# Where the load buffers start: 384 bytes left free ahead of them, and a first load divided at 3968 columns

## The chip, the cores and the metric

The kernel runs on one core of a Trainium2 chip. The metric is the device time of one execution in microseconds; lower is better. Ratios are computed as the mean time of one kernel's fast runs over the mean of the other's fast runs of the same rounds, so they are not quite the ratio of the medians quoted beside them.

## The reference

A cross entropy with label smoothing over 256 rows of 32000 float32 logits, 32.77 MB in all:

```python
log_probs = logits - np.max(logits, axis=-1, keepdims=True)
log_probs = log_probs - np.log(np.sum(np.exp(log_probs), axis=-1, keepdims=True))
# smooth_targets: smoothing / num_classes everywhere, 1 - smoothing more at the label
return (-np.sum(smooth_targets * log_probs, axis=-1)).astype(np.float32)
```

For each row it takes the sum of the logits, the sum of their exponentials and the one logit at the label.

## The kernel before

Each of the 128 partitions holds two rows ("row 0" and "row 1" below). They are loaded in 14 pieces; VectorE sums the logits of a piece and ScalarE its exponentials. Large pieces go into a ring of three buffers of 32000 bytes per partition, small ones into buffers of their own right behind the ring.

```python
WIDTHS = (
    (8000, 8000, 8000, 8000),
    (8000, 6272, 4736, 3648, 2688, 2048, 1536, 1216, 1024, 832),
)
# ...
    ring = ctx.enter_context(tc.tile_pool(name="ring", bufs=3))
    tail = ctx.enter_context(tc.tile_pool(name="tail", bufs=1))
# ...
    def load(w: int, col: int, name: str):
        # ... xt from ring (w >= 4736) or tail
        if col == 0:
            h = w // 2
            nc.sync.dma_start(out=xt[:, :h], in_=x[:, :h])
            nc.scalar.dma_start(out=xt[:, h:w], in_=x[:, h:w])
        else:
            nc.sync.dma_start(out=xt[:, :w], in_=x[:, col : col + w])
        return xt
# ...
        nc.scalar.activation(out=ja[:, :w], in_=xt[:, :w], func=AF.Exp, accum_out=out)
```

A load is 128 descriptors, one per partition, each a contiguous run of up to 32000 bytes; each of the 16 DMA engines carries 8 of them. "A row" below, where DMA is meant, is one such descriptor.

The softmax here doesn't subtract the row's maximum and nothing guards it: scores larger than these inputs give would overflow.

## Time and profile before

| what | value |
|---|---|
| median of 3 runs | 84.77 us (84.75 to 84.93) |
| span of the profiled execution | 83.2 us |
| DMA queues of the loads, share of 16 engines' span | 87.4% + 5.8% |
| ScalarE, VectorE busy | 71%, 45% |
| first byte of the loads moved, last byte moved, last load landed | 1.04, 78.66, 79.11 us |
| last exponential starts | 79.24 us |

How to read it: the DMA engines work without a break from 1.04 to 78.66 us. After the last landing only a short chain is left: the last exponential, its logarithm, a transpose on TensorE, a sum on VectorE, and the store. "Landed" means that the last of the load's 16 engines has reported.

### The profile page before, as it was taken

The page shows a single profiled execution, that of the slowest core. Times are in us where ns is not written, and L with a number is a line of the kernel's source. Part 1 is how long each engine was busy: PE and PEld are TensorE (multiplying, and loading weights), DVE is VectorE, ACT ScalarE, POOL GpSimd, SP SyncE. Part 2 cuts the span into 40 slices and gives each one's busy share as a digit, 9 for nine tenths or more (in the row PEclk, how much of TensorE's full clock was granted, in tenths as well). Part 3 has the DMA queues.
Part 4 walks back from the last instruction along what each step waited for, and adds up shares of the span by engine and source line. Part 5 has one row for each costly group of instructions (what it writes and reads, how often), then busy time and mean ns, then how long its engine had stood idle before and what let it go on. Part 6 is the DMA issues. An engine that isn't in the chain of part 4 may idle for free.

```text
span 83.2 us, 230 instructions
## 1 busy us (share of the span) xinstructions
PE 7.0 (8%) x23; PEld 5.0 (6%) x23; DVE 37.1 (45%) x35; ACT 58.8 (71%) x31; POOL 5.7 (7%) x19
## 2 busy tenths in 40 slices
PE   0000000000000000000000010000000000899020
PEld 0000000000000000000000000000000000787000
DVE  0000005950495009910397017922944736754860
ACT  5000005997499809994399908997999999999960
POOL 3201640031000000000000040000000000000000
PEclk9999999999999999999999999999999999999995
DMA  5999999997999899989998998998999999999600
GB/s 131 416 416 408 454 423 462 477 447 323 477 493 431 369 431 493 446 369 416 493 462 354 416 439 386 495 447 370 428 420 414 442 407 415 412 414 412 256 0 0
DMA packets 2258, 32.77 MB, mean 394 GB/s; under 512 B 337, under 2 KB 338, under 8 KB 850
## 3 DMA queue, kind: packets, MB, share of 16 engines
q1 hardware_dynamic: 2018, 30.72, 87.4%
q10 hardware_dynamic: 144, 2.05, 5.8%
q0 software_dynamic: 96, 0.00, 0.1%
HBM read 32.77 MB, written 0.00 MB: 394 GB/s over the span
## 4 chain that ended last, share of the span: by engine, by line
DMA 64%; ACT 32%; issue 1%; SPq 0%; PE 0%; DVE 0%; ACTq 0%
DMA xt<-in_logits_dram 40%; DMA xl<-in_logits_dram 23%; ACT ja L188 17%; ACT jt L188 15%; SPq L167 0%; PE lse_t L193 0%; DVE res L284 0%; ACT lse L279 0%; ACTq L188 0%
## 5 line engine op out<-in xcount | busy, mean ns | idle before, releaser
L188 ACT ACTIVATE ja<-xt 128x8000 bf16<-128x8000 f32 (+2 forms) x7 | 43.9, 6276 | 20.1 <-DMA xt<-in_logits_dram 20.0
L173 DVE SCALAR_TENSOR_TENSOR jd<-xt 128x4000 f32<-128x4000 f32 (+2 forms) x7 | 27.7, 3954 | 33.6 <-DMA xt<-in_logits_dram 33.6
L188 ACT ACTIVATE jt<-xl 128x3648 bf16<-128x3648 f32 (+6 forms) x7 | 12.2, 1748 | 0.1
L173 DVE SCALAR_TENSOR_TENSOR jd<-xl 128x1824 f32<-128x1824 f32 (+6 forms) x7 | 7.9, 1125 | 5.2 <-DMA xl<-in_logits_dram 5.0
L270 PE MATMUL warm<-xl,ident 128*128 128x256 f32 x20 | 6.1, 471 | 21.4 <-DMA xl<-in_logits_dram 21.4
L270 PEld LDWEIGHTS warm<-xl,ident 128*128 128x128 f32 x20 | 4.8, 246 | 22.5 <-DMA xl<-in_logits_dram 21.7
L193 PE MATMUL loss_t<-ident,loss 128*1 128x128 f32 x1 | 0.4, 372 | 49.2 <-POOL loss L224 49.2
L193 PEld LDWEIGHTS loss_t<-ident,loss 128*1 128x1 f32 x1 | 0.1, 79 | 49.2 <-POOL loss L224 49.2
L226 DVE COPY res<-loss_t 1x128 f32<-1x128 f32 x1 | 0.3, 278 | 4.5 <-PE loss_t L193 4.5
L211 POOL TENSOR_TENSOR half<-sums 128x4 f32<-128x4 f32 x1 | 0.2, 198 | 28.2 <-ACT ja L188 28.2
L125 POOL DMA_INDIRECT gat<-in_logits_dram,flat_idx x2 | 2.0, 1004 | 0.7 <-POOL ident masks.py:199 0.4
L92 ACT ACT_TABLE_LOAD x1 | 1.3, 1283 | 0.9 <-PEq L311 0.9
L188 ACT ACTIVATION_READ_ACCUMULATOR ja<-xt 128x1 f32 x7 | 1.3, 186 | 0.0
L188 ACT ACTIVATION_READ_ACCUMULATOR jt<-xl 128x1 f32 x7 | 1.3, 181 | 0.0
L146 POOL TENSOR_SCALAR weighted<-gat 128x1 f32<-128x1 f32 x1 | 0.8, 763 | 5.8 <-DMA gat<-in_logits_dram,flat_idx 5.8
L105 POOL DMA_DIRECT2D lab<-in_labels_dram x1 | 0.8, 766 | 1.0 <-POOLq L311 1.0
L216 ACT ACTIVATE lse<-half 128x1 f32<-128x1 f32 x1 | 0.2, 203 | 0.6 <-POOL half L211 0.6
L173 DVE DVE_READ_ACCUMULATOR jd<-xt 128x1 f32 x7 | 0.6, 82 | 0.0
L173 DVE DVE_READ_ACCUMULATOR jd<-xl 128x1 f32 x7 | 0.6, 82 | 0.0
L117 POOL TENSOR_TENSOR flat_idx<-rowoff,lab 128x2 int32<-128x2 int32 x1 | 0.2, 197 | 5.4 <-DMA lab<-in_labels_dram 5.4
L193 PE MATMUL lin_t<-ident,done 128*1 128x128 f32 x1 | 0.3, 270 | 3.0 <-DVE done L263 3.0
L282 DVE COPY lin_row<-lin_t 1x128 f32<-1x128 f32 x1 | 0.3, 278 | 0.4 <-PE lin_t L193 0.4
(20 smaller groups left out, 3.8 us busy)
## 6 DMA issues: line engine op xcount, KB each, us to landing
xt<-in_logits_dram SPq DMA_DIRECT2D x4, 4000.0 KB, 21.1
xt<-in_logits_dram SPq DMA_DIRECT2D x1, 3136.0 KB, 19.4
xt<-in_logits_dram SPq DMA_DIRECT2D x1, 2368.0 KB
xt<-in_logits_dram SPq DMA_DIRECT2D x1, 2000.0 KB, 11.5
xt<-in_logits_dram ACTq DMA_DIRECT2D x1, 2000.0 KB, 13.2
xl<-in_logits_dram SPq DMA_DIRECT2D x1, 1824.0 KB, 19.5
xl<-in_logits_dram SPq DMA_DIRECT2D x1, 1344.0 KB, 22.3
xl<-in_logits_dram SPq DMA_DIRECT2D x1, 1024.0 KB, 24.3
```

The source lines that it names most:

```text
L92: nc.scalar.add_instruction(mybir.InstLoadActFuncSet(name=nc.get_next_instruction_name(), act_func_set_id=tbl, ins=[], outs=[],))
L105: nc.gpsimd.dma_start(out=lab[:], in_=labels.bitcast(I32).rearrange("(p f) -> p f", p=P))
L117: nc.gpsimd.tensor_tensor(out=flat_idx[:], in0=rowoff[:], in1=lab[:].rearrange("p (r two) -> p r two", two=2)[:, :, 0:1], op=ALU.add,)
L125: nc.gpsimd.indirect_dma_start(out=gat[:, r : r + 1], out_offset=None, in_=logits[:], in_offset=bass.IndirectOffsetOnAxis(ap=flat_idx[:, r ...
L146: nc.gpsimd.tensor_scalar(out=weighted[r], in0=gat[:, r : r + 1], scalar1=label_weight, scalar2=None, op0=ALU.mult,)
L173: return nc.vector.scalar_tensor_tensor(out=jd[:, :h], in0=xt[:, :h], scalar=1.0, in1=xt[:, h:w], op0=ALU.mult, op1=ALU.add, accum_out=out,)
L188: nc.scalar.activation(out=ja[:, :w], in_=xt[:, :w], func=AF.Exp, accum_out=out)
L193: nc.tensor.transpose(out=row[:], in_=column, identity=ident[:])
L211: nc.gpsimd.tensor_tensor(out=half[:], in0=sums[:, :, :n], in1=sums[:, :, n:], op=ALU.add)
L226: nc.vector.tensor_copy(out=res[:, :, r : r + 1], in_=loss_t[:])
L270: nc.tensor.matmul(warm[:], lhsT=ident[:], rhs=xt[:, i * WARM_COLS : (i + 1) * WARM_COLS], start=True, stop=True,)
L282: nc.vector.tensor_copy(out=lin_row[:], in_=lin_t[:])
```

## The change

Its intent is to let every descriptor of the large loads start on a multiple of 256 bytes, in SBUF and in DRAM. In the built program the ring began at byte 16512 of each partition (64.5 x 256); with 384 bytes of padding ahead of it, it begins at 16896 (66 x 256). The first load was cut at 16000 bytes (62.5 x 256), and is now cut at 15872 (62 x 256).

```diff
+PAD = 384
@@
+    pad = ctx.enter_context(tc.tile_pool(name="pad", bufs=1))
+    pad.tile([nc.NUM_PARTITIONS, PAD // 4], FP32, name="pad", tag="pad")
     ring = ctx.enter_context(tc.tile_pool(name="ring", bufs=3))
@@
-            h = w // 2
+            h = w // 128 * 64
```

## The prediction

> **What bounds the kernel now.** I read the page's span and slices first, then the chain of waits, then the timeline of the last 35 us, then busy times in chosen stretches, and last the packet records of the trace (one per descriptor: start, duration, size). The slices put the 16 DMA engines at nine tenths or more nearly everywhere:
>
> ```profile
> DMA  5999999997999899989998998998999999999600
> ...
> q1 hardware_dynamic: 2018, 30.72, 87.4%
> q10 hardware_dynamic: 144, 2.05, 5.8%
> ```
>
> The two queues of the loads fill 87.4 + 5.8 = 93.2% of 83.15 us, 77.5 us on each engine. By the packet records the first byte of the loads moves at 1.04 us and the last ends at 78.66 us, a stretch of 77.6 us: the DMA engines have no idle time to give back. Only the time per descriptor could shrink. The chain of waits shows who hands over to whom at the end (columns: start us, length us, what):
>
> ```profile
> 20.35 20.37 DMA xt<-in_logits_dram
> 40.72 0.02 issue
> 40.74 0.02 ACTq L188
> 40.76 0.04 issue
> 40.80 6.97 ACT ja L188 x2
> ...
> 48.17 19.52 DMA xl<-in_logits_dram
> 67.69 0.02 issue
> 67.72 7.63 ACT jt L188 x5
> ```
>
> Up to 67.69 us the landing of loads sets the pace; from 67.72 us on ScalarE does, without a pause, until 80.2 us. The timeline shows how close the two are (start, duration, instruction, in brackets the idle time before it):
>
> ```profile
> 50.31 6.87 ACT L188 ACTIVATE ja<-xt 128x8000 bf16<-128x8000 f32 x1 [1.75 <-DMA xt<-in_logits_dram]
> ...
> 57.77 5.43 ACT L188 ACTIVATE ja<-xt 128x6272 bf16<-128x6272 f32 x1 [0.50 <-DMA xt<-in_logits_dram]
> ...
> 63.41 4.15 ACT L188 ACTIVATE ja<-xt 128x4736 bf16<-128x4736 f32 x1
> ...
> 67.72 3.24 ACT L188 ACTIVATE jt<-xl 128x3648 bf16<-128x3648 f32 x1
> ...
> 70.96 2.44 ACT L188 ACTIVATE jt<-xl 128x2688 bf16<-128x2688 f32 x1
> ```
>
> Set beside them when each load landed, by the trace's semaphore records: the 3648-column load landed at 67.69 us and its exponential began at 67.72; for the six that follow the pairs are 70.94 and 70.96, 73.42 and 73.44, 75.31 and 75.39, 76.82 and 76.90, 78.10 and 78.18, 79.11 and 79.24. The widths were tuned so that each load lands just as ScalarE needs it. A DMA that gets faster therefore meets ScalarE at once.
>
> The rate of the DMA in stretches that hold one load size each (columns: stretch, its length, busy time and instructions of PE, weight loads, DVE, ACT, POOL, then clock, DMA share, GB/s):
>
> ```profile
> 21.00:49.00 28.00, 0.00 (x0) 0.00 (x0) 13.00 (x6) 21.09 (x7) 0.82 (x5) 1.00 0.99 427
> ...
> 67.30:69.90 2.60, 0.00 (x0) 0.00 (x0) 2.07 (x2) 2.54 (x3) 0.00 (x0) 1.00 0.98 414
> ...
> 74.90:75.80 0.90, 0.90 (x6) 0.77 (x6) 0.40 (x1) 0.90 (x3) 0.00 (x0) 1.00 1.01 410
> ```
>
> The engines are full in all three, and the rate falls as rows get shorter (32000, 10752, 4864 bytes): each descriptor carries something fixed besides its bytes.
>
> **What the Trainium skill says.** "DMA: Bandwidth & Descriptors", section "Where 436 GB/s comes from", gives 16 ports x 32 bytes x 850 MHz = 435 GB/s. The trace agrees: between rows of 8192 and 25088 bytes the median duration rises from 313 to 935 ns, 622 ns for 16896 bytes or 528 beats of 32 bytes, 1.178 ns a beat, which is 849 MHz. So no change of addresses can lift the rate above about 435, and the large loads already run at 427. Section "How a descriptor splits into AXI transactions" says that a descriptor which starts on a 256-byte boundary goes out as pieces of 256 bytes, and that one which doesn't starts its first piece at the boundary below, whose unused bytes still cost beats. "SBUF — State Buffer", section "SBUF: two separate sides", says that DMA and engines use disjoint ports, so I expect no effect of moved addresses on compute; no run here shows that yet.
>
> **The change part by part.** The order of instructions on every engine is the same in both builds, with the same sizes except for the two first transfers. So nothing is removed or added; only addresses move. In the built program the load buffers begin at byte 16512 of each partition, 128 bytes past a multiple of 256. With the pad they begin at 16896, a multiple of 256 (and of 512). The other ring buffers lie 32000 bytes apart (125 x 256), and all widths of row 1 are multiples of 64 columns (256 bytes), so before, every load's destination sat 128 bytes off, and after, every one is aligned. The sources in DRAM were aligned already, but for the first load's second half (16000 bytes is 62.5 x 256), which the division at 3968 (62 x 256 bytes) mends. After it the two parts are 62 and 63 whole pieces.
>
> What is an off-boundary descriptor charged? A row of n pieces that starts 128 bytes off touches n + 1 of them. If each touched piece takes a full 8 beats, a descriptor takes 8(n+1) beats. I took durations in beats (1.176 ns) from the packet records: 25088 bytes (n = 98) takes 935 ns = 794.8, against 8 x 99 = 792; 18944: 709 ns = 602.7 against 600; 14592: 549 = 466.7 against 464; 10752: 408 = 346.8 against 344; 8192: 313 = 266.1 against 264; 4864: 191 = 162.4 against 160; 16000 (63 pieces touched on either half): 596 = 506.6 against 504; 32000: 1186 = 1008.1 against 1008. One rule with a rest of 2 to 3 beats (none at 32000) fits halves and whole rows alike. A plain "bytes plus a constant" needs 10.7 beats at 14592 but 6.6 at 16000. I take the rule of touched pieces, as my estimate. Aligned, each row then saves one piece, 8 beats = 9.4 ns.
>
> Each engine has 8 rows of every load, so each load saves 8 x 9.4 = 75 ns; the divided first load saves one piece for each pair of halves, also 75 ns. The saving at the landing of each load adds up: first load 0.08 us, fifth load (row 1's 8000 columns) 0.38, 6272 columns 0.45, 4736 columns 0.53, 3648 columns 0.60, 2688 columns 0.68, 2048 columns 0.75, the last (832) 14 x 0.075 = 1.05. (These are 14 loads; the last lands at 79.11 - 1.05 = 78.06.)
>
> What ScalarE makes of it, carrying its own durations: 8000 columns begin at 50.31 - 0.38 = 49.93 and end about 56.8. The 6272 columns land for 57.77 - 0.45 = 57.32 and end at 62.75. The 4736 columns begin at 63.41 - 0.53 = 62.88 and end at 67.03. The 3648 columns begin at 67.72 - 0.60 = 67.12. The 2688 columns would have landed for 70.28, but ScalarE is free only at 67.12 + 3.24 = 70.36. From there ScalarE alone sets the end; its seven activations follow on one another as before, and the gain stays at 0.60 us plus whatever of the waits of 0.02 to 0.06 us between them goes, at most 0.1. The remaining 0.45 us of DMA time is gained where no one waits for it. Sum: 84.77 - 0.60 to 0.70 = 84.1 to 84.2 us.
>
> **The rivals.** First, a fixed cost: the 6 to 10 beats per row could be what any descriptor costs, aligned or not. For it: every row before the change starts off a boundary on one side, so nothing in this trace shows an aligned one. Against it: the misfit of 16000 against 14592 bytes above. It would leave 84.77. Second, half of it: if the cut first and last pieces together are charged only 4 beats extra, the saving at the 3648-column load is 0.30 us, and the time 84.45. Third, the whole saving reaches the end, were ScalarE not there: 84.77 - 1.05 = 83.7. Against it: ScalarE's unbroken row from 67.72 us. Fourth, the pad moves the buffers that the engines write and read, and slows VectorE or ScalarE; nothing speaks for it, and a loss of 1% in ScalarE's 12.5 us tail is 0.13 us. A large gain is excluded by the beat: if every beat beyond the bytes went up to the 3648-column load (6.6 for each half, 8 for 32000 bytes, 10.7 for three later sizes, 8 rows each), that is 8 x (13.2 + 32 + 32.1) = 618 beats = 0.73 us.
>
> **Range and chances.** I give the touched pieces two chances in three, half of it and the fixed cost the rest, and lean a little towards them: 84.2 us, and 83.9 to 84.8 eight times in ten. Faster by over 2% would need 83.1 us, more than the whole saving of the DMA: 2%. Slower by over 2%: 1%. Within 2%: 97%.
>
> **What would show it.** Packet durations: 32000-byte rows at 1176 to 1179 ns instead of 1186, 25088 at 926 instead of 935, 4864 at 181 instead of 191; the halves at about 586 and 596. The rate in the large loads near 430 to 433. The loads' last packet about 1.05 us earlier, near 77.6; the 3648-column exponential at 67.1, and VectorE in the tail starting before ScalarE on the same tile, as its data is there sooner. ScalarE's durations unchanged (6870 ns for 8000 columns). Wrong if durations stay (fixed cost), if rows shorten but another gap opens between them, or if any activation gets longer.

## The result, and the profile after

84.34 us (median of 6, 84.28 to 84.56) against 84.78 (median of 6 of the same rounds): ratio 0.9951, 95% interval 0.9937 to 0.9966. That is a gain of 0.44 us, clear of noise and inside 2%. It lies inside the predicted range; the point forecast was 84.2.

The page's lines for the DMA, after: as full as before, the same shares of a span that is 0.6 us shorter.

```profile
span 82.6 us, 230 instructions
...
DMA  5999999996999799979997999998999999999600
...
q1 hardware_dynamic: 2018, 30.71, 87.4%
q10 hardware_dynamic: 144, 2.06, 5.9%
```

The chain of waits, after (start, length, what). Compare 67.72 and 67.31 for the first piece of the tail, and the shape of what follows:

```profile
57.45 5.52 ACT ja L194 x2
...
63.05 4.24 ACT ja L194 x2
...
67.31 7.53 ACT jt L194 x5
74.83 0.06 issue
74.89 1.40 ACT jt L194
76.29 0.07 issue
76.36 1.22 ACT jt L194 x2
```

The five entries that took 7.63 us before take 7.53. ScalarE looked unbroken before, but it had been stretched by pauses of hundredths of a microsecond. By the instruction records these were 42, 35 and 24 ns ahead of the exponentials of 2048, 1536 and 1216 columns, and none in the changed kernel. (The `issue` entries of the chain begin at a semaphore and do not measure a pause.) The timeline has the ends of the tail; first the kernel before, then the changed one (start, duration, instruction):

```profile
70.96 2.44 ACT L188 ACTIVATE jt<-xl 128x2688 bf16<-128x2688 f32 x1
...
73.44 1.91 ACT L188 ACTIVATE jt<-xl 128x2048 bf16<-128x2048 f32 x1
...
75.39 1.49 ACT L188 ACTIVATE jt<-xl 128x1536 bf16<-128x1536 f32 x1
...
76.90 1.22 ACT L188 ACTIVATE jt<-xl 128x1216 bf16<-128x1216 f32 x1
...
79.24 0.88 ACT L188 ACTIVATE jt<-xl 128x832 bf16<-128x832 f32 x1
```

```profile
70.55 2.43 ACT L194 ACTIVATE jt<-xl 128x2688 bf16<-128x2688 f32 x1
...
72.98 1.91 ACT L194 ACTIVATE jt<-xl 128x2048 bf16<-128x2048 f32 x1
...
74.89 1.47 ACT L194 ACTIVATE jt<-xl 128x1536 bf16<-128x1536 f32 x1
...
76.36 1.20 ACT L194 ACTIVATE jt<-xl 128x1216 bf16<-128x1216 f32 x1
...
78.68 0.88 ACT L194 ACTIVATE jt<-xl 128x832 bf16<-128x832 f32 x1
```

The lead over the kernel before grows along the tail: 0.41 us at 2688 columns, 0.46 at 2048, 0.50 at 1536, 0.54 at 1216, 0.56 at 832. Had ScalarE alone set the pace in the kernel before, the lead would have stayed at 0.41. The pauses that went give 0.10 us of the growth, and three exponentials that are 12 to 17 ns shorter, for a reason that the trace does not show, the rest. The last landing moved by as much as the last exponential: from 79.11 to 78.55 us. (These two profiled executions differ by 0.57 us, the medians by 0.44; the stage up to the end of the second load, which varies from run to run, gives 0.12 us of it here.)

The rate in the stretches that the prediction quotes reads 422, 426 and 422 GB/s after, against 427, 414 and 410. These stretches count a packet where it starts, so their edges hide a change of half a per cent; the packet records do not. From them I take the time per row: from the mean end of a load on the 16 engines to the mean end of the next one, divided by 8. In nanoseconds, and with it the time from the end of a load's last data to its landing:

```
bytes of a row              32000   25088   18944   14592    4864
before, ns per row         1185.2   931.9   706.1   545.9   190.0
after,  ns per row         1181.9   928.4   701.9   542.0   186.1
                                            14592-byte load   last load
last data to landing, before                     451 ns        443 ns
last data to landing, after                      324 ns        331 ns
```

Two things changed: a row goes through 3 to 4 ns faster on the average, and the report of a landed load comes 0.12 us sooner. (By this table the 32000-byte loads ran at 16 x 32000 / 1185.2 = 432 GB/s before and at 433 after; the prediction's 427 came from the edges of its stretch.) In single packets the median of a 25088-byte row fell from 935 to 931 ns, not to the predicted 926. The records also show what kind of cost it was. After, all 128 rows of the 14592-byte load took exactly 545 ns. Before, 30 of them took 545 ns too, and the others 546 to 556: rows were held up at times, by nothing that a row of its own size or address explains.

### The profile page after: what moved, and what is told of

It reads as the page before. It is cut to its first block, busy times and chain, and to the rows that moved or that the text cites. A ratio compares the mean times of both kernels' runs of the same rounds, so it can differ in the third digit from the quotient of the medians.

```text
span 82.6 us, 230 instructions
## 1 busy us (share of the span) xinstructions
PE 7.0 (8%) x23; PEld 5.0 (6%) x23; DVE 37.1 (45%) x35; ACT 58.7 (71%) x31; POOL 6.2 (7%) x19
## 4 chain that ended last, share of the span: by engine, by line
DMA 59%; ACT 35%; issue 1%; SPq 0%; PE 0%; DVE 0%; ACTq 0%
DMA xt<-in_logits_dram 59%; ACT ja L194 20%; ACT jt L194 15%; SPq L173 0%; PE lse_t L199 0%; DVE res L290 0%; ACT lse L285 0%; ACTq L194 0%
## 5 line engine op out<-in xcount | busy, mean ns | idle before, releaser
L152 POOL TENSOR_SCALAR weighted<-gat 128x1 f32<-128x1 f32 x1 | 1.2, 1193 | 5.3 <-DMA gat<-in_logits_dram,flat_idx 5.3
```

Of the source, the lines that this page charges most:

```text
L152: nc.gpsimd.tensor_scalar(out=weighted[r], in0=gat[:, r : r + 1], scalar1=label_weight, scalar2=None, op0=ALU.mult,)
```

## The experiments

Theory A, formed from this: a row whose place in SBUF starts off a multiple of 256 bytes costs about 4 ns more, and delays the report by 0.12 us; the source and the division don't matter. Its rivals are named with each run. All kernels passed the comparison with the reference; so did the two that leave out work, as 640 missing exponentials of 32000 move the logarithm too little for its tolerance. Each was timed in five rounds beside the kernel before.

**The pad alone.**

```diff
-            h = w // 128 * 64
+            h = w // 2
```

> The pad alone, the first load still divided at 4000 columns. Theory A (a destination that starts off a 256-byte boundary costs its row about 4 ns, and the landing notice about 0.12 us more): rows of 25088 bytes at 931 ns, 4864 at 187, as in the changed kernel, last load landing near 78.55 us; only the second half of the first load is off a boundary, 8 rows x 4 ns = 0.03 us, so 84.3 to 84.45 us. Rival B (the division of the first load is what helped, by an earlier first stage): 84.7 to 84.8 us.

Measured: 84.30 us against 84.83, ratio 0.9937 (0.9919 to 0.9955). 14592-byte rows at 545 ns, all 128. The pad alone gives at least the whole gain. The last load landed at 78.78 us, not near 78.55; the profiled execution was the slowest of its six, 84.61 us.

**The division alone**, on the kernel before.

```diff
-            h = w // 2
+            h = w // 128 * 64
```

> The division at 3968 columns alone, no pad. Theory A: rows of 25088 bytes stay at 935 ns, 4864 at 191, last load landing near 79.1 us; 84.7 to 84.85 us. Rival B: 84.3 to 84.5 us.

Measured: 84.83 us against 84.83, ratio 0.9997 (0.9983 to 1.0011). The two parts of the first load took 592 and 601 ns a row (15872 and 16128 bytes), in sum 1193, where the equal halves took 596 + 596 = 1192. Rival B falls: the division does nothing, although one half had both its addresses off a boundary in the kernel with the pad alone (it took 596 ns there too). The run also shows an exception to theory A: both parts have a destination 128 bytes off here (16512, and 16512 + 15872 = 126.5 x 256), and their rows take the same 592 and 601 ns as in the changed kernel, where both are aligned. In the first load the charge does not show.

**128 bytes of pad in place of 384.**

```diff
-PAD = 384
+PAD = 128
```

> 128 bytes of pad instead of 384, with the division at 3968: buffers start on multiples of 256, but what was a multiple of 512 is now 256 off it and the other way round. Theory A (256 is the boundary): as the changed kernel, 84.3 to 84.45 us, 25088-byte rows at 931 ns. Rival C (512 is the boundary for some buffers): row durations that differ between buffers, 84.4 to 84.7 us.

Measured: 84.30 us, ratio 0.9932 (0.9917 to 0.9947); 928.3 ns per 25088-byte row. The buffers that were on a multiple of 512 are now 256 off it, and nothing changes: 256 is enough, and rival C falls.

**256 bytes of pad**: everything is moved, but stays 128 off.

```diff
-PAD = 384
+PAD = 256
```

> 256 bytes of pad, with the division at 3968: everything is moved, but still 128 bytes off a multiple of 256. Theory A: as the kernel before, 84.7 to 84.85 us, 25088-byte rows at 935 ns. Rival D (any move away from the old place helps, for instance by other SBUF banks for engines and DMA): 84.3 to 84.5 us.

Measured: 84.83 us, ratio 1.0001 (0.9985 to 1.0018); 931.8 ns per 25088-byte row, report after 472 ns in the 14592-byte load. Moving alone does nothing; rival D falls. With these four runs theory A stands.

**How far off the boundary.** The same pad line with 416, 448 and 608 bytes puts the buffers 32, 64 and 224 bytes past a multiple of 256. This asks what is charged: unused bytes ahead of the start, or the fact of being off.

> Load buffers 32 bytes past a multiple of 256 (pad 416), otherwise as the changed kernel. Theory A1 (a row that starts anywhere off the boundary costs one more piece on the write side, 8 beats, which hides the 4 beats every row pays anyway: plus 4 beats, whatever the distance): 25088-byte rows take 932 ns per row from load to load as in the kernel before, 84.75 to 84.9 us. Theory A2 (only the unused bytes ahead of the start cost beats, one per 32 bytes): 1 beat, 929.5 ns per row, 84.4 to 84.55 us.

> Load buffers 224 bytes past a multiple of 256 (pad 608). Theory A1: the same as 128 bytes or 32 bytes off, 932 ns per 25088-byte row, 84.75 to 84.9 us. Theory A2: 7 beats ahead of the start, 936.5 ns per 25088-byte row, 85.1 to 85.4 us. A third way (only a boundary of 32 or 64 bytes matters, or the last piece counts): as the changed kernel, 84.3 us.

> Load buffers 64 bytes past a multiple of 256 (pad 448). After the runs at 32 and 224 bytes off, which cost 933 ns per 25088-byte row against 932 at 128 bytes: theory E1 (any start off 256 costs the whole piece, a start off 128 one beat more): 933 ns and 84.9 to 85.05 us, slightly above the kernel before. Theory E2 (the extra beat is for starts off 64 bytes): 932 ns and 84.75 to 84.95 us.

Measured, with the 128-byte case for comparison (times per row as above; against its own runs of the kernel before):

```
bytes off       0 (after)   32      64      128 (pad 256)   224
25088, ns         928.4    932.9   931.9      931.8        932.8
18944, ns         701.9    707.2   706.2      706.1        707.2
ratio            0.9951   1.0019  1.0014      1.0001       1.0020
95% low          0.9937   1.0000  0.9998      0.9985       1.0001
95% high         0.9966   1.0037  1.0029      1.0018       1.0039
```

32 and 224 bytes cost the same, so theory A2 (a beat for each unused 32 bytes) falls: it wanted 929.5 and 936.5 ns. The charge is for being off, whatever the distance, as A1 has it; the medians, 85.01 us at 32 bytes and 85.02 at 224, are 0.1 us above what A1 allowed. In these two row sizes a further nanosecond separates 32 and 224 from 64 and 128; 64 bytes off cost what 128 do, which fits theory E2, that the extra one goes with starts off a multiple of 64. It is not settled: the 14592-byte rows took 548.2, 547.4, 545.8 and 547.0 ns at 32, 64, 128 and 224 bytes, which puts 64 bytes beside 224. In time that nanosecond is not resolved either: the median at 64 bytes, 85.11 us, is above what E1 and E2 allowed, and its interval takes in both readings.

**The source off the boundary.** Buffers aligned as in the changed kernel, but the columns shifted by 32, so that most loads read from 128 bytes past a multiple of 256 in DRAM.

```diff
-    (8000, 8000, 8000, 8000),
-    (8000, 6272, 4736, 3648, 2688, 2048, 1536, 1216, 1024, 832),
+    (7968, 8000, 8000, 8032),
+    (7968, 6272, 4736, 3648, 2688, 2048, 1536, 1216, 1024, 864),
-        xt = ring.tile([P, max(WIDTHS[0])], FP32, name="xt", tag="xt")
+        xt = ring.tile([P, RING_COLS], FP32, name="xt", tag="xt")   # RING_COLS = 8064
```

> Buffers aligned as in the changed kernel, but most columns of DRAM read from 128 bytes off a multiple of 256 (first load of each row 32 columns narrower, last one 32 wider). Theory S1 (the read side is charged for the piece too): 25088-byte rows at about 932 ns per row instead of 928, but the landing notice early as in the changed kernel, 84.7 to 84.9 us. Theory S2 (only the write side is charged): 928 ns, 84.3 to 84.5 us.

Measured: 84.40 us against 84.89, ratio 0.9956 (0.9931 to 0.9982). 928.0 ns per 25088-byte row, 542.1 per 14592-byte row, as with aligned sources. Theory S1 falls: the source's start costs nothing that the pace shows.

**Both off**: the same columns in the kernel before.

> Source and destination both 128 bytes off (the kernel before with the shifted columns). If the sides run beside each other and the slower one sets the pace: 25088-byte rows at 932 ns per row as in the kernel before, 84.75 to 84.95 us. If the charges add: 936 ns, 85.1 to 85.4 us. If equal offsets cancel (pieces passed on one to one): 928 ns, 84.3 to 84.5 us.

Measured: 84.92 us, ratio 1.0014 (0.9991 to 1.0038); 931.6 ns per 25088-byte row. Equal offsets don't cancel and charges don't add. As the source alone is free, this says no more than that the destination decides here too.

**Who sets the end.** The prediction held that from the 3648-column tile on ScalarE alone sets the end. Then freeing ScalarE must bring the end forward. In the changed kernel the exponential of that tile leaves out 640 columns, a wrong result:

```diff
+        v = w - 640 if w == 3648 else w
-        nc.scalar.activation(out=ja[:, :w], in_=xt[:, :w], func=AF.Exp, accum_out=out)
+        nc.scalar.activation(out=ja[:, :v], in_=xt[:, :v], func=AF.Exp, accum_out=out)
```

> The changed kernel with 640 columns fewer in the exponential of the 3648-column tile (result wrong on purpose), which frees ScalarE 0.54 us before the last six tiles. Theory F (the prediction's: from that tile on ScalarE alone sets the end, the last loads have 0.45 us to spare): the last exponential starts 0.4 to 0.5 us earlier, 83.85 to 83.95 us. Theory G (each load lands just when ScalarE needs it, the last landing holds the end): at most 0.1 us earlier, 84.2 to 84.4 us, the last exponential starting about 0.09 us after the last landing.

Measured: 84.49 us against 84.85, ratio 0.9947 (0.9933 to 0.9961). That is no faster than the changed kernel (0.9951). The timeline shows where the freed half microsecond went: into a wait for the next load, in the brackets of the second line.

```profile
67.48 2.71 ACT L195 ACTIVATE jt<-xl 128x3008 bf16<-128x3008 f32 x1
...
70.69 2.44 ACT L195 ACTIVATE jt<-xl 128x2688 bf16<-128x2688 f32 x1 [0.40 <-DMA xl<-in_logits_dram]
...
78.83 0.88 ACT L195 ACTIVATE jt<-xl 128x832 bf16<-128x832 f32 x1
```

The last load landed at 78.70 us, 0.13 us ahead of the last exponential. Theory F falls: the next load had no 0.45 us to spare. Of the two G stands, although its 84.2 to 84.4 us was missed by 0.09. That the last landing alone holds the end is more than the trace shows, though. In the changed kernel five of the six exponentials after the 3648-column one start as the one before them ends, and 0.02 to 0.14 us after their own load landed; only the one of 1024 columns pauses, 0.065 us, and follows its landing. From the 2688-column tile on, the two are level to about 0.1 us.

**The same cut in the kernel before.**

> The same cut of 640 columns in the kernel before (result wrong on purpose). Theory G: at most 0.1 us earlier than the kernel before, 84.7 to 84.8 us, and later than the same cut in the changed kernel by the last landing's 0.4 to 0.55 us. Theory F: 84.25 to 84.5 us.

Measured: 84.95 us, ratio 1.0003 (0.9990 to 1.0017), and the same new wait in its timeline:

```profile
67.60 2.71 ACT L189 ACTIVATE jt<-xl 128x3008 bf16<-128x3008 f32 x1
...
70.86 2.44 ACT L189 ACTIVATE jt<-xl 128x2688 bf16<-128x2688 f32 x1 [0.45 <-DMA xl<-in_logits_dram]
...
79.13 0.88 ACT L189 ACTIVATE jt<-xl 128x832 bf16<-128x832 f32 x1
```

In both kernels half a microsecond less of ScalarE at this place is worth nothing. In the pair the last exponentials are 0.30 us apart, the last landings 79.02 - 78.70 = 0.32, the ratios 0.0056, which is 0.48 us of 84.85. What I expected for this run, 84.7 to 84.8, was a little low.

**An attempt to go lower.** If the last landing and the exponential behind it set the end, a narrower last load should help.

```diff
-    (8000, 6272, 4736, 3648, 2688, 2048, 1536, 1216, 1024, 832),
+    (7936, 6080, 4736, 3520, 2560, 1984, 1472, 1216, 960, 832, 704),
-WARM_LEFT, WARM_COLS = 5, 256
+WARM_LEFT, WARM_COLS = 6, 256
```

> An attempt to use the shorter landing: the changed kernel with row 1 in eleven loads whose last is 704 columns wide instead of 832 (widths 7936, 6080, 4736, 3520, 2560, 1984, 1472, 1216, 960, 832, 704). If the last landing plus the last exponential sets the end: the last exponential is 128 columns or 0.11 us shorter, one more load costs the DMA about 0.05 us; so 0.06 us earlier than the changed kernel, 84.2 to 84.35 us. If ScalarE set the end: one more activation costs it 0.18 us, and the time rises to 84.45 to 84.6 us.

Measured: 84.71 us against 84.78, ratio 0.9993 (0.9980 to 1.0007): slower than the changed kernel, and above both expected ranges. The expected part came: the store was issued 0.05 us earlier (first the changed kernel, then this one):

```profile
80.58 0.32 SPq L298 DMA_DIRECT2D out_dram<-res  x1
```

```profile
80.53 0.32 SPq L298 DMA_DIRECT2D out_dram<-res  x1
```

But the program ends with a fixed list of waits on SyncE for the semaphores of the transfers, two to an instruction and about 0.06 us an instruction. With one load more the store got a semaphore that stands in the second instruction of this list, not in the last. In the instruction records of the changed kernel the store lands at 81.71 us and the list is done at 81.75. Here it lands at 81.66, and the four waits that were still to be worked off end at 81.93. The waits of SyncE show it from the other side (us waited, times, longest), the changed kernel first:

```profile
SPq L331 <- DMA out_dram<-res: 0.5, 1, 0.5
```

```profile
SPq L331 <- DMA out_dram<-res: 0.7, 1, 0.7
```

That accounts for 0.17 us of span (81.93 - 81.75 at that point, 82.8 against 82.6 at the end); the medians are 0.37 us apart, and the rest stays open. No version beat the changed kernel clearly; 128 bytes of pad do as well as 384, and the division can go.

## Why the prediction was right or wrong

- **What bounds the kernel** was right: the DMA engines have no idle time, only the time per descriptor could shrink, and it did.
- **Addresses move, compute stays** was right. A ScalarE activation over 8000 columns took 6870 ns before and 6872 after, a VectorE sum 4325 and 4326.
- **A row saves one whole piece, 8 beats or 9.4 ns**: this step failed in its size. Measured are 3.3 to 4.2 ns, about 3 to 3.5 beats, in the rows of 14592 bytes and more (table above). From the end of the second load to that of the last the data took 57.39 to 57.44 us in the four kernels 128 bytes off (before, division alone, pad 256, and the unpadded one with the cut), and 57.06 to 57.16 us in the four aligned ones (after, pad alone, pad 128, and the padded one with the cut). The means differ by 0.31 us over 12 loads, where the prediction had 12 x 0.075 = 0.90. Its second rival, half a piece (4 beats, 4.7 ns), was the nearest in size, and its 84.45 us in time. The fit went wrong because it assumed that an aligned row costs its bytes and 2 to 3 beats of rest. It costs more: in the fit's own measure, the median duration, an aligned 14592-byte row takes 545 ns or 463 beats, 7 above the 456 of its bytes. From load to load, where successive rows overlap a little, it takes 542.0 ns or 460.7 beats, 4.7 above, of which about one is the 9-ns report shared by 8 rows. The Trainium skill has a cost of this kind, in "DMA: Bandwidth & Descriptors", section "Why small descriptors are slow (HBM only)": a fixed overhead of about 3 cycles per packet. I passed over it. The 3.7 beats left here are of that size; that they are the same cost, no run shows. Whether being off costs a whole piece of which half hides behind that overhead, or half a piece, the runs do not settle. That it is not the unused bytes ahead of the start, they do.
- **The first load saves one piece by the division** was wrong: 1193 ns for both parts against 1192, no change of time in the run of the division alone, and no loss in the run of the pad without it. (Nor did every load's destination sit 128 bytes off before: the second half of the first load began at 16512 + 16000 = 127 x 256.)
- **ScalarE sets the end from the 3648-column tile, and 0.45 us of the DMA's gain is lost**: wrong. The two runs with a lighter exponential show it. ScalarE and the landings were so closely matched that I read its row as unbroken, where in the kernel before the loads still held it up by hundredths of a microsecond. The tell was in the timeline: 70.96 + 2.44 = 73.40, and the next exponential starts at 73.44, just after its load's landing at 73.42. In the profiled pair the whole gain of the DMA reached the end: the last landing and the last exponential both moved by 0.56 us. Right in this step was that the pauses would go; they and the shorter exponentials gave 0.15 us, where it allowed 0.1. The error here and the one of size worked against each other, so that 84.2 came close by luck: a small saving in every load from the third to the last, all of it used, in place of 8 loads at a large one.
- **The signs that it named**: ScalarE's durations stayed. The others came smaller than forecast: rows of 32000 bytes at 1185 ns (1176 to 1179 forecast), of 4864 bytes at 187 (181), parts of the first load at 592 and 601 (586 and 596), the last packet at 78.22 us (77.6), the 3648-column exponential at 67.31 (67.1). VectorE started before ScalarE in the last four tiles, by 0.005 to 0.11 us, where it had done so in the last two.
- **Not foreseen at all**: the report of a landed load comes 0.12 us sooner. In the 14592-byte load it takes 443 to 476 ns after the last data in all eight kernels that are off, and 289 to 371 ns in all five that are aligned. With the 0.31 us of data that makes about 0.43 us, against 0.44 us between the medians. A picture that fits both is that the writing side of an off-boundary load falls behind the reading side, so that rows are held up now and then and the report waits; the rows of 545 ns among the slower ones, and halves of the first load that cost nothing while the queue was young, speak for it. It is argued, not shown.
- **A fixed cost that alignment can't touch**, the first rival, and **slower engines**, the fourth, are refuted by the run with the pad alone and by the durations above. The pad also moves the engines' own buffers behind the ring, in every run alike; as the engines' durations stayed while the DMA's rows shortened, these are not the cause.

## What to carry to other kernels

In a kernel bound by loads, look at the byte address at which the load buffers start in SBUF: here a start off a multiple of 256 cost some 4 ns a descriptor and 0.12 us at each landing, and leaving 128 bytes free ahead of the buffers removed both. It is half a per cent at rows of 32 KB; the rows of 4864 bytes lost 2% of their time to it, 190.0 ns against 186.1. And where two engines hand over without a gap, take work away from one of them before calling it the bound.

## What the Trainium skill lacked or had wrong

- "DMA: Bandwidth & Descriptors", section "How a descriptor splits into AXI transactions": it speaks of transactions that read, and of unused bytes ahead of the start. Here a source 128 bytes off cost nothing that the pace shows (928.0 ns per 25088-byte row against 928.4), and a destination off cost 4.5 and 4.4 ns whether 32 or 224 bytes ahead were unused (932.9 and 932.8 ns).
- The same page states no effect of a destination's start on the landing report; the runs show about 0.12 us (324 ns after the last data against 451).
- The same page, section "Why small descriptors are slow (HBM only)", works out its fixed overhead of about 3 cycles for a 256-byte descriptor alone. It has no number for large ones: at rows of 14592 bytes 4.7 beats beyond the bytes are left here, about one of them the report.
- "SBUF — State Buffer", section "Operand start alignment", is about legality and says that nothing was timed; the cost of a start off 256 bytes is the number that it lacks, 0.44 us in 84.8 here.
- No page has the list of closing waits: a store whose semaphore stands early in it ended the program later, by 0.17 us here.
